# Modulation products of a two-layer diffusion backbone: 512 moving columns instead of four times 128

## The chip, the core and the metric

The kernel runs on one core of one Trainium2 chip. The metric is the device time of one execution in microseconds (us), the median of several runs. A core has five engines with instruction streams of their own: TensorE (PE in the rows; its weight loads are PEld), VectorE (DVE), ScalarE (ACT), GpSimd (POOL) and SyncE (SP, which only issues DMA transfers here). A DMA transfer is issued on an engine's queue and carried out by 16 shared DMA engines.

## What is computed

The reference runs two layers on 512 latent tokens and 256 context tokens of width 1024. Layer 0 mixes tokens by multi-head latent attention, layer 1 by a bidirectional gated linear recurrence; each is followed by a SwiGLU feed-forward part. Both sub-layers of a layer are normed and modulated:

```python
mod_l = jnp.split((jax.nn.silu(c) @ ada_w[i] + ada_b[i])[:, None, :], N_MOD, axis=-1)
mod_c = jnp.split((jax.nn.silu(c_ctx) @ ada_w[i] + ada_b[i])[None, None, :], N_MOD, axis=-1)
a_l = modulate(rms_norm(x, norm1_w[i]), mod_l[0], mod_l[1])
...
x = x + mod_l[2] * o_l
```

The change concerns the first two lines: two vectors (c and c_ctx, width 1024) times a weight matrix `ada_w[i]` of 1024 x 6144, for each of the two layers, in float32. Its 6144 outputs are shifts, scales and gates.

## The kernel before

Activations lie feature-major: a feature tile is 128 features on the 128 partitions, with tokens along the free axis. Most products of the kernel are split by hand into a high and a low part of each factor and taken as three products (`mm3`, lines 93 to 99; `mm3m`, lines 101 to 110); their lines are 97 to 99 and 108 to 110. A weight tile comes through a ring: `weight` (lines 72 to 85) takes a buffer of tag "wf" (1024 columns, four buffers), loads it by a transfer on SP, and makes the high part on ScalarE (L83) and the low part on GpSimd (L84).

The modulation is computed by `ada` (lines 150 to 168), in calls of four chunks of 128 outputs. A layer has 48 chunks, so there are twelve calls a layer and 24 in all. The vectors SiLU(c) and SiLU(c_ctx) lie in `s32`: for each feature tile k of eight, 128 x 32, of which two columns are used. For each chunk i the call takes a buffer of the same ring "wf" and loads 512 KB: all eight feature tiles of one chunk, side by side (L155). Then it makes eight products, one per feature tile (L158): stationary `s32[:, k, :]` with 32 columns, moving 128 columns of the weights, in plain float32, which the chip runs as two instructions. The product of feature tile k writes the 32 partitions that begin at 32 * (k % 4) of the bank, so it uses the strip of 32 array columns with number j = k % 4:

```python
j = k % 4
nc.tensor.matmul(rows_ps[32 * j:32 * j + 32, i * P:(i + 1) * P], lhsT=self.s32[:, k, :],
                 rhs=w[:, k * P:(k + 1) * P], start=(k < 4), stop=(k >= 4))
```

The bank is then copied to SBUF by ScalarE (L161), transposed by TensorE in four pieces (L164), and VectorE sums the four strips and adds the bias (L166, L168).

The calls stand here: four for the first norm of layer 0, while the inputs are loaded (L341, L352, L353); ten spread over the heads of the attention (L543, chunks by `ADA_HEAD`, the last four of them layer 1's); two before the feed-forward part of each layer (L679); two at the first norm of layer 1 (L318); three after the last head of the recurrence (L893, by `ADA_HG`) and one at its output (L854, by `ADA_O`).

The order of each engine's instructions isn't the order of the code. The program is built with `schedule_with_timeline_sim=True` (L1124): a scheduler plays the program through and gives each engine, whenever it would be free, the ready instruction of highest priority. Products of `ada` in the attention have their priority lowered (`PRIO`, "ada_m"), so they are put where the scheduler finds nothing else ready. An engine then runs its own list strictly in the order given, on the chip.

`pack` (lines 1066 to 1113) lays out the inputs on the host. `cols(w, n)` (L1070) cuts a matrix into blocks of n output columns and puts each block's feature tiles side by side; for the modulation n is 128 (L1082), so that a chunk is one block of 512 KB in memory.

Of the kernel before, what the change touches and what calls it, by code (L numbers as in the profile page):

```python
# [17 lines left out]
P = 128  # L18
D = 1024
KD = D // P  # L20
# [22 lines left out]
RING = 1024  # L43
# [12 lines left out]
class Kernel:  # L56
# [93 lines left out]
    def ada(self, l, u0, n, pool, bank):  # L150
        nc = self.nc
        rows_ps = bank()
        for i in range(n):
            w = self.ring.tile([P, RING], F32, tag="wf", name="adaw", bufs=4)
            nc.sync.dma_start(out=w[:, :D], in_=self.a["ADA"][l, u0 + i])  # L155
            for k in range(KD):
                j = k % 4
                nc.tensor.matmul(rows_ps[32 * j:32 * j + 32, i * P:(i + 1) * P], lhsT=self.s32[:, k, :],  # L158
                                 rhs=w[:, k * P:(k + 1) * P], start=(k < 4), stop=(k >= 4))
        rows = pool.tile([P, 512], F32, tag="adarow", name="rows", bufs=1)  # L160
        nc.scalar.copy(rows[:, :n * P], rows_ps[:, :n * P])  # L161
        tp = bank()
        for i in range(n):
            nc.tensor.transpose(tp[:, i * P:(i + 1) * P], rows[:, i * P:(i + 1) * P], self.ident)  # L164
        s = pool.tile([P, 4, 2], F32, tag="adas", name="adas", bufs=2)
        nc.vector.tensor_reduce(s[:, :n], tp[:, :n * P].rearrange("p (u j c) -> p u c j", u=n, j=4)[:, :, 0:2, :], axis=AX.X, op=ALU.add)  # L166
        b = self.vec[:, VEC_AB + l * 48 + u0:VEC_AB + l * 48 + u0 + n]
        nc.vector.tensor_tensor(self.mod[l][:, u0:u0 + n, :], s[:, :n], b.unsqueeze(2).broadcast_to([P, n, 2]), op=ALU.add)  # L168
# [407 lines left out]
    def bank(self, ps):  # L576
        return ps.tile([P, 512], F32, tag="q", name="q", bufs=5)
# [488 lines left out]
def pack(i):  # L1066

    f = {k: np.asarray(v) for k, v in i.items()}

    def cols(w, n):  # L1070

        k, m = w.shape
        return np.ascontiguousarray(w.reshape(k // P, P, m // n, n).transpose(2, 1, 0, 3)).reshape(m // n, P, k // P * n)

    def vec(v):
        return v.reshape(-1, P).T

    d = {}
    xt = np.concatenate([f["x"][0], f["ctx"][0]], 0)
    d["XT"] = np.ascontiguousarray(xt.T.reshape(KD, P, NT).transpose(1, 0, 2))  # L1080
    d["CC"] = np.ascontiguousarray(np.stack([vec(f["c"][0]), vec(f["c_ctx"])], -1))
    d["ADA"] = np.stack([cols(f["ada_w"][l], P) for l in range(2)])  # L1082
    d["VEC"] = np.ascontiguousarray(np.concatenate(
        [vec(f["norm1_w"].ravel()), vec(f["norm2_w"].ravel()), vec(f["ada_b"].ravel()),
         vec(f["hg_lb_logits"].ravel()), f["hg_o_norm_w"][0].reshape(P, 1)], 1))
    d["BC"] = np.concatenate([f["mla_q_norm_w"][0], f["mla_kv_norm_w"][0], f["mla_qn_w"][0], f["mla_kn_w"][0],
                              f["mla_qr_w"][0], f["mla_kr_w"][0]])
    d["WIN"] = np.ascontiguousarray(f["mla_w_in"][0].reshape(KD, P, 704).transpose(1, 0, 2))
    d["WUP"] = np.ascontiguousarray(np.concatenate(
        [cols(f["mla_w_uq"][0], 384), cols(f["mla_w_ukv"][0], 256).reshape(H // 2, 2, P, 512).transpose(0, 2, 1, 3).reshape(H // 2, P, 1024)], 2))  # L1090
    d["MWO"] = cols(f["mla_w_o"][0], P)
    d["W1"] = np.stack([cols(f["ffn_w1"][l], P) for l in range(2)])
    d["W3"] = np.stack([cols(f["ffn_w3"][l], P) for l in range(2)])
    d["W2"] = np.stack([cols(f["ffn_w2"][l], P) for l in range(2)])
    wi = f["hg_w_in"][0]
    d["HW"] = np.stack([cols(wi[:, m * D:(m + 1) * D], P) for m in (0, 1, 2, 4)])
    d["HWI"] = cols(wi[:, 3 * D:4 * D], 256)
    d["HWO"] = cols(f["hg_w_o"][0], P)

    s, t = np.meshgrid(np.arange(32), np.arange(32), indexing="ij")  # L1100
    lv = [s == t] + [(s // (2 * b) == t // (2 * b)) & (s // b != t // b) for b in (1, 2, 4, 8, 16)]
    d["MSK"] = np.ascontiguousarray(np.tile(np.stack(lv, 1), (4, 1, 1)).astype(np.float32))

    row = np.repeat(np.arange(NL // 64, dtype=np.float32), 64)
    col = np.tile(np.arange(64, dtype=np.float32), NL // 64)
    inv = np.power(np.float32(10000.0), -np.arange(0, 32, 2, dtype=np.float32) / np.float32(32)).astype(np.float32)
    ar, ac = row[:, None] * inv, col[:, None] * inv
    ang = np.concatenate([ar, ar, ac, ac], -1)
    cos = np.concatenate([np.cos(ang), np.ones((NC_, DR))], 0)
    sgn = np.tile(np.repeat(np.array([-1.0, 1.0]), 16), 2)  # L1110
    sin = np.concatenate([np.sin(ang) * sgn, np.zeros((NC_, DR))], 0)
    d["ROPE"] = np.ascontiguousarray(np.stack([cos, sin], 1).reshape(TT, P, 2, DR).transpose(1, 0, 2, 3).astype(np.float32))
    return d
# [15 lines left out]
```

## Time and profile before

| what | value |
|---|---|
| median of three runs | 1847.92 us (1844.15 to 1857.01) |
| the profiled execution | 1853.65 us |
| its span, first to last instruction | 1851.9 us |
| TensorE busy | 1755.5 us, 95% of the span |
| VectorE, ScalarE, GpSimd busy | 1016.3, 762.6, 760.6 us |
| mean granted clock of TensorE | 0.982 of full speed |

The rows further down come from the profiled execution. In them L158 is line 158 of the kernel, `out<-in` names the tile written and the tiles read, and x16 the number of instructions that one row sums up. Products are pipelined, so the duration of one holds its way through the array, and rows of the timeline overlap a little. Where an engine sat idle ahead of a row, the idle time and what ended it stand in brackets.

### The profile page before, as it was taken

To read this page: it belongs to the slowest core of one execution; us is meant where nothing else is said; L and a number is where in the kernel's file an instruction comes from. 1 tells how busy PE (TensorE), PEld (TensorE's weight loads), DVE (VectorE), ACT (ScalarE), POOL (GpSimd) and SP (SyncE) were. 2 spreads that over 40 slices of the span, in tenths; PEclk is the share of its full clock that TensorE was granted. 3 is DMA by queue.
4 is the path that set the end of the run, shared out by engine and by line. 5 is a ranking of instruction groups with operands and counts; after the bars stand their busy time and mean duration, and the time that the engine had idled before them with its cause. 6 is when DMAs were issued, how large, how long until landed. Compare 5 with 4: busy or idle time off the path is not lost. (4 is left out here: it accounts for less than half of the span.)

```text
span 1851.9 us, 33106 instructions
## 1 busy us (share of the span) xinstructions
PE 1755.5 (95%) x13708; PEld 1591.8 (86%) x13708; DVE 1016.3 (55%) x1646; ACT 762.6 (41%) x1467; POOL 760.6 (41%) x528
## 2 busy tenths in 40 slices
PE   4889999999899999999999999999998889999999
PEld 3878989788799999988887888888896779999888
DVE  5567887741754445432203666575745278888400
ACT  4355565532554344432213332423333255555411
POOL 2333342216566666643344554554643440000442
PEclk9999999999999999999999999999999989999999
DMA  7412032523222322254224121111115233333331
GB/s 268 137 39 73 25 116 98 170 74 122 103 86 97 104 96 103 81 168 136 86 71 148 60 69 47 61 55 58 58 35 191 94 137 103 103 115 103 108 118 49
DMA packets 55015, 183.61 MB, mean 99 GB/s; under 512 B 6224, under 2 KB 8528, under 8 KB 54864
## 3 DMA queue, kind: packets, MB, share of 16 engines
q1 hardware_dynamic: 53424, 173.62, 28.5%
q10 hardware_dynamic: 1440, 7.86, 1.2%
q8 instruction: 108, 1.77, 0.4%
q14 instruction: 43, 0.35, 0.1%
HBM read 171.50 MB, written 9.96 MB: 98 GB/s over the span
## 5 line engine op out<-in xcount | busy, mean ns | idle before, releaser
L84 POOL TENSOR_TENSOR wl<-wf,wh 128x1024 fp32r<-128x1024 f32 (+2 forms) x130 | 287.0, 2214 | 438.9 <-ACT wh L83 436.5
L83 ACT CAST wh<-wf 128x1024 fp32r<-128x1024 f32 (+2 forms) x130 | 122.9, 947 | 226.2 <-PE L L98 102.5
L97 PE MATMUL q<-op,sh 128*128 128x384 f32 (+1 forms) x640 | 197.3, 310 | 1.0 <-ACT sh L622 1.0
L98 PE MATMUL q<-op,sh 128*128 128x384 f32 (+1 forms) x640 | 197.6, 310 | 0.0
L99 PE MATMUL q<-op,sl 128*128 128x384 f32 (+1 forms) x640 | 194.9, 310 | 0.0
L97 PEld LDWEIGHTS q<-op,sh 128*128 128x128 f32 x640 | 120.3, 188 | 1.5 <-ACT sh L622 1.5
L98 PEld LDWEIGHTS q<-op,sh 128*128 128x128 f32 x640 | 120.3, 188 | 0.0
L99 PEld LDWEIGHTS q<-op,sl 128*128 128x128 f32 x640 | 119.5, 188 | 0.0
L623 POOL TENSOR_TENSOR sl<-wf,sh 128x1024 fp32r<-128x1024 f32 (+1 forms) x40 | 88.7, 2218 | 56.4 <-ACT sh L622 56.4
L98 PE MATMUL L<-op,sh 128*128 128x256 f32 (+1 forms) x360 | 110.4, 307 | 0.0
L99 PE MATMUL L<-op,sl 128*128 128x256 f32 (+1 forms) x360 | 110.3, 306 | 0.0
L97 PE MATMUL L<-op,sh 128*128 128x256 f32 (+1 forms) x360 | 110.3, 306 | 0.0
L1060 DVE TENSOR_TENSOR X<-X,T 128x512 f32<-128x512 f32 x96 | 78.1, 855 | 47.0 <-PE lv L985 45.9
L557 DVE SCALAR_TENSOR_TENSOR xl<-L,mod,xl 128x512 f32<-128x512 f32 x24 | 17.9, 750 | 153.8 <-PE L L99 149.8
L622 ACT CAST sh<-wf 128x1024 fp32r<-128x1024 f32 x80 | 66.7, 834 | 70.2 <-PE L L98 32.7
L98 PE MATMUL L<-f_lo,wh 128*128 128x512 f32 (+1 forms) x240 | 89.1, 371 | 0.0
L97 PE MATMUL L<-f_hi,wh 128*128 128x512 f32 (+1 forms) x240 | 89.0, 371 | 0.0
L99 PE MATMUL L<-f_hi,wl 128*128 128x512 f32 (+1 forms) x240 | 88.5, 369 | 0.0
L158 PE MATMUL L<-adaw,s 128*32 128x128 f32 x1216 | 57.1, 297 | 29.5 <-DMA adaw<-in_ADA 29.3
L975 POOL TENSOR_SCALAR km<-X 128x512 f32<-128x512 f32 x40 | 29.4, 737 | 125.5 <-DVE X L1060 76.4
L622 ACT CAST sh<-sb 128x1024 fp32r<-128x1024 f32 x40 | 42.0, 1050 | 88.5 <-PE q L98 46.6
L158 PEld LDWEIGHTS L<-adaw,s 128*32 128x32 f32 x1216 | 34.8, 116 | 46.1 <-DMA adaw<-in_ADA 17.2
(466 smaller groups left out, 5585.3 us busy)
## 6 DMA issues: line engine op xcount, KB each, us to landing
wf<-in_W SPq DMA_DIRECT2D x104, 512.0 KB, 3.5
adaw<-in_ADA SPq DMA_DIRECT2D x96, 512.0 KB, 4.4
wf<-in_HW SPq DMA_DIRECT2D x32, 512.0 KB, 3.5
wf<-in_W SPq DMA_DIRECT2D x24, 384.0 KB, 3.2
gd<-s SPq DMA_DIRECT2D x10, 768.0 KB, 3.5
g<-gd ACTq DMA_DIRECT2D x10, 768.0 KB, 4.7
wf<-in_W SPq DMA_DIRECT2D x16, 320.0 KB, 3.0
wf<-in_MWO SPq DMA_DIRECT2D x8, 512.0 KB, 4.1
```

What stands on the lines that cost most here:

```text
L83: nc.scalar.copy(hi[:, :n], w[:, :n])
L84: nc.gpsimd.tensor_sub(lo[:, :n], w[:, :n], hi[:, :n].bitcast(F32))
L97: nc.tensor.matmul(out, lhsT=lh, rhs=rh, start=(new and i == 0), stop=False, skip_group_check=more)
L98: nc.tensor.matmul(out, lhsT=lh, rhs=rl, start=False, stop=False, skip_group_check=more)
L99: nc.tensor.matmul(out, lhsT=ll, rhs=rh, start=False, stop=(i == n - 1), skip_group_check=more)
L158: nc.tensor.matmul(rows_ps[32 * j:32 * j + 32, i * P:(i + 1) * P], lhsT=self.s32[:, k, :], rhs=w[:, k * P:(k + 1) * P], start=(k < 4), sto ...
L557: nc.vector.scalar_tensor_tensor(xk, po, gate[:, s:s + 1], xk, op0=ALU.mult, op1=ALU.add)
L622: nc.scalar.copy(hi[:, :n], s)
L623: (nc.vector if j in on_dve else nc.gpsimd).tensor_sub(lo[:, :n], s, hi[:, :n].bitcast(F32))
L975: nc.gpsimd.tensor_scalar(km.rearrange("p (m b r) -> p m b r", b=2, r=L), mix, 1.0, 0.0, op0=ALU.mult, op1=ALU.add)
L1060: nc.vector.tensor_tensor(v, v, t, op=ALU.mult)
```

## The change

The weights are laid out in blocks of 512 output columns, and a call of four chunks is one block. A buffer of the ring now holds two feature tiles of all four chunks in place of eight feature tiles of one chunk. For each feature tile one product takes 512 moving columns. The strip is still k % 4, and the transfers are still four a call with 512 KB each; a partition's part of a transfer is 4 KB in one piece, and the pieces of neighbouring partitions lie 16 KB apart.

```diff
     def ada(self, l, u0, n, pool, bank):
         nc = self.nc
         rows_ps = bank()
-        for i in range(n):
+        g, c0 = divmod(u0, 4)
+        src = self.a["ADA"][l, g].rearrange("p (k c) -> p k c", k=KD)[:, :, c0 * P:(c0 + n) * P]
+        kn = RING // (n * P)
+        for k0 in range(0, KD, kn):
             w = self.ring.tile([P, RING], F32, tag="wf", name="adaw", bufs=4)
-            nc.sync.dma_start(out=w[:, :D], in_=self.a["ADA"][l, u0 + i])
-            for k in range(KD):
+            nc.sync.dma_start(out=w.rearrange("p (k c) -> p k c", k=kn), in_=src[:, k0:k0 + kn])
+            for k in range(k0, k0 + kn):
                 j = k % 4
-                nc.tensor.matmul(rows_ps[32 * j:32 * j + 32, i * P:(i + 1) * P], lhsT=self.s32[:, k, :],
-                                 rhs=w[:, k * P:(k + 1) * P], start=(k < 4), stop=(k >= 4))
+                nc.tensor.matmul(rows_ps[32 * j:32 * j + 32, :n * P], lhsT=self.s32[:, k, :],
+                                 rhs=w[:, (k - k0) * n * P:(k - k0 + 1) * n * P], start=(k < 4), stop=(k >= 4))
...
-    d["ADA"] = np.stack([cols(f["ada_w"][l], P) for l in range(2)])
+    d["ADA"] = np.stack([cols(f["ada_w"][l], 4 * P) for l in range(2)])
```

## Rows read from the trace of the kernel before

**Rows 1.** The page: busy time, share of the span and instructions by engine.

```profile
PE 1755.5 (95%) x13708; PEld 1591.8 (86%) x13708; DVE 1016.3 (55%) x1646; ACT 762.6 (41%) x1467; POOL 760.6 (41%) x528
```

**Rows 2.** Busy by stage: PE, PEld, DVE, ACT, POOL; then clock, DMA share, GB/s.

```profile
0.00:56.00 56.00, 32.20 (x354) 23.93 (x354) 27.14 (x55) 22.58 (x39) 14.06 (x15) 0.94 0.81 270
...
130.00:370.00 240.00, 229.54 (x2027) 203.00 (x2026) 190.22 (x442) 138.13 (x345) 80.90 (x96) 0.98 0.29 100
...
463.00:476.00 13.00, 9.67 (x151) 6.28 (x150) 9.44 (x20) 4.69 (x9) 2.10 (x2) 0.99 0.77 271
...
1395.00:1418.00 23.00, 18.13 (x441) 14.05 (x439) 13.33 (x25) 9.41 (x23) 3.60 (x6) 0.93 0.70 237
```

**Rows 3.** Busy time by stage, L158 alone: PE, then PEld.

```profile
130.00:370.00 240.00, 31.59 (x640) 18.78 (x640) 0.98 0.29 100
...
sum 1852.00, PE 69.91 PEld 43.28; mean PE 5.83 PEld 3.61
```

**Rows 4.** Timeline of TensorE in the attention: start, duration, line, count.

```profile
173.57 0.28 PE L98 MATMUL L<-wl,cn_hi 128*128 128x256 f32 x1
173.69 0.28 PE L99 MATMUL L<-wh,cn_lo 128*128 128x256 f32 x1
173.90 0.41 PE L158 MATMUL L<-adaw,s 128*32 128x128 f32 x2
...
176.18 0.64 PE L158 MATMUL L<-adaw,s 128*32 128x128 f32 x14
177.12 0.41 PE L158 MATMUL L<-adaw,s 128*32 128x128 f32 x2
...
177.93 1.08 PE L158 MATMUL L<-adaw,s 128*32 128x128 f32 x32
...
179.26 0.64 PE L158 MATMUL L<-adaw,s 128*32 128x128 f32 x14
```

**Rows 5.** The same timeline at 353 to 358 us, runs of other lengths.

```profile
353.53 0.42 PE L158 MATMUL L<-adaw,s 128*32 128x128 f32 x6 [0.80 <-DMA adaw<-in_ADA]
...
354.35 0.41 PE L158 MATMUL L<-adaw,s 128*32 128x128 f32 x4
...
357.31 0.62 PE L158 MATMUL L<-adaw,s 128*32 128x128 f32 x10
```

**Rows 6.** Timeline of TensorE at layer 0's second norm.

```profile
468.71 1.13 PE L215 MATMUL q<-dg,ones 128*128 128x512 f32 x2
470.37 0.64 PE L158 MATMUL L<-adaw,s 128*32 128x128 f32 x16 [0.53 <-DMA adaw<-in_ADA]
470.94 0.70 PE L215 MATMUL q<-dg,ones 128*128 128x256 f32 x2
...
474.41 0.65 PE L158 MATMUL L<-adaw,s 128*32 128x128 f32 x16 [2.02 <-DMA adaw<-in_ADA]
474.98 0.62 PE L108 MATMUL q<-op,wh 128*128 128x384 f32 x2
```

**Rows 7.** The first and the last run of L158 in TensorE's timeline.

```profile
17.03 2.28 PE L158 MATMUL L<-adaw,s 128*32 128x128 f32 x32 [17.03 <-DMA adaw<-in_ADA]
...
1493.53 0.64 PE L158 MATMUL L<-adaw,s 128*32 128x128 f32 x16
```

**Rows 8.** Waits of TensorE: us in total, times, longest.

```profile
PE L L158 <- DMA adaw<-in_ADA: 29.3, 11, 17.0
```

**Rows 9.** SP's waits, two DMA issues, and the first transfers' rate (last column).

```profile
SPq L155 <- PE L L158: 102.3, 27, 37.3
...
adaw<-in_ADA SPq DMA_DIRECT2D x96, 512.0 KB, 4.4
...
wf<-in_WIN SPq DMA_DIRECT2D x8, 352.0 KB, 4.0
...
2.00:10.00 8.00, 0.00 (x0) 0.00 (x0) 2.75 (x10) 5.70 (x10) 0.00 (x0) 1.00 0.87 273
10.00:20.00 10.00, 2.85 (x36) 1.97 (x36) 5.58 (x12) 4.68 (x10) 0.00 (x0) 1.00 0.91 324
```

## The prediction, made before the change was run

> **What bounds the kernel now.** I read the page first, then TensorE's busy time by stage, then the order of its instructions around the line that changes, then the waits.
>
> The page has TensorE busy for 95% of the span, no other engine over 55% [rows 1]. So a microsecond that TensorE gains or loses is mostly a microsecond of the kernel, unless it falls where TensorE waits anyway. The products of the change (L158) are 1536 instructions, two for each of 768 float32 products, the two passes over the same columns.
>
> By stage, the attention stretch has TensorE busy 229.5 of 240 us: bound by TensorE. The short stretch at layer 0's second norm, 463 to 476 us, has it busy three quarters of the time, with the DMA engines at 77%: there the modulation weights pace the work. There are six such places, of which three stretches are shown [rows 2]. L158 alone is busy 69.9 us: 31.6 in the attention stretch, for ten of the 24 calls, and 38.3 in the other fourteen [rows 3]. That is 3.16 and 2.74 us a call.
>
> The timeline shows how a call runs. It isn't one block: the scheduler cuts it and puts the pieces between other products. The call at 174 us comes as 2, 14, 2, 32 and 14 instructions [rows 4]. Over the program I count 86 such runs, 3.6 to a call; the first and the last are shown [rows 7]. And the length of a run is a staircase. A run of 2 instructions (one product) takes 0.41 us, of 4 takes 0.41, of 6 takes 0.42; then 10 take 0.62, 14 take 0.64, and 32 take 1.08 [rows 4, 5]. One product and three cost the same. Products of four feature tiles go to four different strips of 32 array columns (j = k % 4 in the code), and the strips work at once; a run lasts as long as the strip with most to do. 16 more instructions, four more per strip, cost 0.44 us.
>
> Is that the streaming of columns, or a price of each instruction? The broadcast product of the norm answers it: two passes over 512 columns take 1.13 us, over 256 columns 0.70 [rows 6]. 0.43 us for 2 x 256 columns is 0.84 ns a column and pass. A strip's four passes over 128 columns at that rate are 0.43 us, and the staircase says 0.44. So L158 is bound by columns streamed per strip, at four strips; loading and issuing are hidden behind it.
>
> **The change, part by part.** It keeps the 24 calls, the 96 transfers of 512 KB, the copy of the rows, the four transposes and the sums. It replaces 32 products of 128 columns per call by 8 of 512. The columns streamed are the same.
>
> *An uncut call.* Before, 64 instructions in one run would take 0.64 + 3 x 0.44 = 1.96 us. After, 16 instructions, two products for each strip: the first four products take 0.41 + 2 x 384 x 0.84 ns = 1.06 us, and four more add 2 x 512 x 0.84 ns = 0.86, in all 1.92. Gain 0.04 us a call, 1 us over 24: nothing.
>
> *A cut call.* Here the change loses. A narrow unit held all eight feature tiles, so every tile that arrived, and every piece of eight products, kept four strips busy. After, a piece of one, two or three wide products keeps one, two or three strips busy, and costs 1.06 us as four would. A weight tile now holds two feature tiles, so a piece of one tile uses half the strips. By pieces per call: one piece 1.92 us; two even pieces 2.12, two uneven ones 1.06 + 1.92 = 2.98; three pieces 3.18; four pieces 4.24.
>
> *How many pieces.* The trace of before cannot show this, since the schedule is worked out anew. From below: one piece. From above: eight, every product alone, 8.5 us a call. The nearest rows are today's 3.6 runs. Runs of a single narrow product [rows 4] may vanish or become a whole wide one; a gap that took 7 or 16 narrow products takes 2 or 4 wide ones. I take 3.5 pieces in the attention stretch: midway between 3.18 and 4.24, 3.71 us, plus 0.3 for waits inside runs, which stay (ten calls, 43 runs by 0.2 and 40 units by 0.44 make 26 of the 31.6 us): 4.0 against 3.16, so +0.85 us a call and +8.5 for ten. A run also costs idle time ahead of it: 0.21 us lie between the start of the product before it and its own, where 0.12 is usual [rows 4], some 0.1 us; eight runs fewer give 0.8 back. That leaves 7.7, and as TensorE is busy 229.5 of 240 us there, a little slack takes some: +6.
>
> *The stretches paced by transfers.* There a run starts when its weights land: TensorE waited 29.3 us for them, 17.0 of it before its first instruction [rows 8]. At 474.41 a unit of 16 runs behind such a wait of 2.02 us, and the layer's first feed-forward product follows it 0.57 us later [rows 6]. After, the last tile of a call holds two wide products: 1.06 instead of 0.64, +0.43 us behind the last landing. The first tile of a call is also released later, by the same 0.43, and the ring of four buffers lets SP issue the next call's transfers only on such releases: SP waited 102 us for L158 [rows 9]. Five places have two or more calls on end at the pace of transfers (two in the first 56 us, then from 463 us, at layer 1's first norm, and from 1395 us; the sixth, layer 1's second norm, is left out since the feed-forward weights follow late there too) [rows 2]. 5 x 0.86 = 4.3, part of it beside the norm's own chain: +4. Queued behind the waiting issue on SP are the weights of the next products, which share the ring; they move by the same 0.4 us.
>
> *The transfers themselves.* As many, as large; a partition's 4 KB stay in one piece, now 16 KB apart in memory. The weights of the input projection are read in rows that lie apart as well and land in 4.0 us, the modulation weights of before in 4.4 [rows 9]. Cost 0; if the pieces were halved to 2 KB, the bound is below.
>
> *Everything else.* 1152 fewer matrix products and as many fewer weight loads to issue: no row shows TensorE waiting for issue in these runs beyond what the staircase holds, so 0. The new durations also reorder the whole schedule around the calls; I have no row for the sign of it and put it into the range, some 5 us either way.
>
> *Sum.* +6 and +4: 10 us. The profiled execution took 1853.65 us for a span of 1851.9, so it would become 1864; it lies 5.7 us above the median of the three runs, 1847.92, to which I refer the forecast: 1858 us.
>
> **The rivals.**
>
> *Torn apart by tile.* Slower. The order waits for each weight tile and puts other products between, as it does with today's units of 16 at 468 to 475 us [rows 6]. Four pieces a call of 1.06 us, two strips idle in each. In the attention stretch 10 x (4.24 + 0.3 - 3.16) = 14; in the other calls 14 x (4.24 + 0.3 - 2.74) = 25, of which the waits for transfers hide about half. 26 to 39 us: 1874 to 1887. It decides from about four pieces a call on. For it: a tile is the unit in which work becomes ready. Against it: four buffers hold a whole call, and in the attention stretch they have mostly landed before a run begins.
>
> *Fewer pieces.* Long products fill a gap that short ones filled in several goes. At two even pieces a call 2.12 + 0.3 = 2.4 us, against 3.16: -7 us in the attention stretch, nothing elsewhere, with the runs saved -9: 1839 (elsewhere the waits for transfers hide it). At one piece everywhere 24 x (2.91 - 2.22) = 17 us less, and 6 for 62 runs fewer: 1825. Against it: what cuts the runs today is other work becoming ready, and that is still there.
>
> *A wide product costs less than four narrow ones.* The change would then do what its form suggests. If a strip's 512 columns took half of what four times 128 take, a call would lose 0.87 us of its 1.74 and 24 calls 21 us: 1827. The row against it is the broadcast product at 0.84 ns a column [rows 6], the same rate as the staircase. The Trainium skill, TensorE: Matmul & The Clock Gate, section "Back-to-back issue gap", gives sustained spacings of about 81 ns for 128 columns and 131 ns for 512, by which a wide product costs 1.6 narrow ones. By that page 24 calls would save about 25 us (estimate), and this case's trace disagrees with it for float32.
>
> *Transfers in pieces of 2 KB.* While the inputs came in 2 KB and 1 KB pieces, the core moved 273 GB/s, with the 4 KB weights 324 [rows 9]. A call's 2.1 MB would take 7.7 instead of 6.5 us; for 14 paced calls at most 17 us: 1865. The layout speaks against it.
>
> **How the numbers follow.** Forecast (about three to four pieces, +2 to +18 us) 0.50; torn apart by tile 0.28; fewer pieces 0.13; wide products cheaper 0.05; smaller transfer pieces 0.04. A measurement of this kernel can tell about 1%, 18.5 us, from no change. Slower by more: the torn case and half of the last, 0.30. Faster by more: cheaper products and the far end of fewer pieces, 0.07. Within: 0.63. The range goes from two even pieces (1839) to the torn case without hiding (1887), less what lies at its ends: 1838 to 1885. The likeliest case alone reaches from 1850 to 1866.
>
> **What would show it.** L158 with 384 products' instructions of 128x512 in place of 1536; runs of 2 to 8 instructions lasting about 1.06 us, of 16 about 1.92. If runs of 16 last near 1.1, the strips did not set the price and I am wrong in the main step. The sum of L158's busy time should rise from 69.9 to about 80; if it falls under 60, the calls run in fewer pieces; if it is near 100, they are torn by tile. The attention stretch should be longer by some 6 us, the stretches at the norms by under 1 each, the feed-forward stretches unchanged. Transfers should land in 4.4 us as before.

## The result, and the profile after

| kernel | median of its runs | ratio to the kernel before, runs of one job | 95% interval |
|---|---|---|---|
| before (12 runs) | 1844.81 us (1839.04 to 1857.01) | 1 | |
| changed (12 runs) | 1861.72 us (1853.01 to 1870.09) | 1.0089 | 1.0065 to 1.0114 |
| changed, later on another chip (e11, 7 runs) | 1859.60 us (1855.82 to 1865.64) | 1.0081 | 1.0051 to 1.0110 |

The change costs 0.8 to 0.9%, 15 to 17 us. The forecast was 1858 us and slower by 10. The profiled execution of the changed kernel took 1868.63 us, 7 us above its own median; that of the kernel before lay 9 us above its median in these runs. So both were profiled a second time (e0 and e11), and what follows rests on what the two profiles of a kernel share. TensorE's mean granted clock was 0.982 and 0.985 of full speed before, 0.984 and 0.985 after: the loss isn't the clock's.

The page of the changed kernel, for [rows 1] and the transfers of [rows 9], and its costliest group of the changed product, which is L161 now (after the arrow: idle time ahead of the group, and what ended most of it):

```profile
PE 1762.3 (94%) x12556; PEld 1560.8 (84%) x12556; DVE 1021.3 (55%) x1646; ACT 763.2 (41%) x1467; POOL 763.4 (41%) x528
...
L161 PE MATMUL L<-adaw,s 128*32 128x512 f32 x304 | 58.1, 629 | 24.5 <-DMA adaw<-in_ADA 24.3
...
adaw<-in_ADA SPq DMA_DIRECT2D x96, 512.0 KB, 4.6
```

1152 instructions fewer, as the change says, and TensorE busy 6.8 us longer (6.7 between the two second profiles). The transfers land in 4.6 us, not 4.4.

TensorE's timeline of the changed kernel, runs of L161:

```profile
44.05 1.05 PE L161 MATMUL M<-adaw,s 128*32 128x512 f32 x4
...
45.70 1.05 PE L161 MATMUL M<-adaw,s 128*32 128x512 f32 x4
...
48.20 1.05 PE L161 MATMUL M<-adaw,s 128*32 128x512 f32 x4
...
173.18 1.92 PE L161 MATMUL L<-adaw,s 128*32 128x512 f32 x16
```

The step costs are those of the forecast to 0.01 us: two products 1.05 (forecast 1.06), eight 1.92 (1.92). A tile that comes alone costs 1.05 where it cost 0.64 [rows 6]. A whole call costs what it did: no call of the kernel before ran uncut, but one of the narrow calls of e4 did, in 1.95 us.

How often a call is cut came out the other way round from the forecast in the attention. The ten calls there ran in 43 pieces before and run in 20 now, 2.0 a call; four of the ten run in one piece. The other fourteen calls, at the transfers' pace, went from 43 to 35 pieces, and 19 of the 35 are single tiles of 1.05 us (one took 1.92 us at the lower clock level). Busy time by stage, columns as in [rows 3]: L158 alone, kernel before (two stages that [rows 3] left out), then L161 alone, changed kernel, in the same stages:

```profile
0.00:56.00 56.00, 12.12 (x256) 7.28 (x256) 0.94 0.81 270
...
1000.00:1015.00 15.00, 5.29 (x128) 3.20 (x128) 1.00 0.72 258
```

```profile
0.00:60.00 60.00, 17.11 (x64) 2.34 (x64) 0.94 0.77 250
...
134.00:374.00 240.00, 26.46 (x160) 4.51 (x160) 0.99 0.31 104
...
1006.00:1022.00 16.00, 6.13 (x32) 0.98 (x32) 1.00 0.73 244
...
sum 1866.00, PE 72.61 PEld 11.79; mean PE 6.05 PEld 0.98
```

In the attention 31.6 us of [rows 3] became 26.5: 5.1 us gained. In the other fourteen calls 69.9 - 31.6 = 38.3 became 72.6 - 26.5 = 46.1: 7.8 us lost, 5.0 of them in the first 60 us. The second profiles have 30.6 and 28.5 us in the attention, 37.4 and 46.8 in the other calls. Two pieces of the 28.5 ran at the lower clock level; with the time lost to that level taken off, the gain in the attention is 4.7 us in the first pair of profiles and 4.1 in the second.

The 5.1 us gained in the attention are not in the kernel's time. All of TensorE's work in that stretch, changed kernel (columns as in [rows 2], where it was busy for 229.5 of 240 us):

```profile
134.00:374.00 240.00, 223.64 (x1533) 186.24 (x1534) 192.86 (x440) 139.65 (x345) 87.34 (x98) 0.99 0.31 104
```

TensorE is busy 5.9 us less in 240 us (5.0 between the second profiles; a little of it because the window holds 14, then 6, other products fewer), and the stretch isn't shorter. What it waits for (us in total, times, longest), first before, then changed, in that stretch:

```profile
PE M L489 <- DVE qk_hi L492: 5.0, 2, 3.7
...
PE sc L514 <- ACT p L524: 0.2, 1, 0.2
```

```profile
PE sc L517 <- ACT p L527: 4.1, 5, 1.9
PE M L492 <- DVE qk_hi L495: 3.2, 3, 1.7
...
PE M L492 <- DVE nm L524: 2.5, 1, 2.5
PE M L492 <- ACT p L527: 1.9, 1, 1.9
PE tp L533 <- DVE pt_lo L536: 1.8, 3, 0.8
```

The wait for qk_hi was there before, and one of 1.9 us for pt_lo too. New or longer are the other waits for the softmax's chain on ScalarE and VectorE (nm, p and pt_lo, L524 to L536). All rows of this view add up to 12.5 us before and 17.7 after, in the second profiles to 9.5 and 15.0: 5.2 and 5.5 us more, about what the pieces gained. In the second profile the waits at L517, L492 for nm and L533 are 3.7, 2.5 and 1.9 us, where e0 has 0.2 and none; that of L492 for p is 1.35 us there, and put down to qk_hi.

Had the narrow pieces stood in these gaps? At six of the waits for nm, p and pt_lo of 0.3 us and more, 7.0 us together, they had: in the kernel before, a narrow piece runs directly ahead of the product that now waits. The longest, before and after:

```profile
338.02 0.85 PE L158 MATMUL L<-adaw,s 128*32 128x128 f32 x22
338.81 0.33 PE L489 MATMUL M<-ident,arena 128*128 128x128 f32 x1
```

```profile
346.27 0.33 PE L492 MATMUL M<-ident,arena 128*128 128x128 f32 x1 [2.46 <-DVE nm L524]
```

Run in larger blocks, the call takes less time, and these gaps stand empty. At three more waits, 3.7 us, no piece had run in the 5 us ahead of the product; these come with the new order of the other products. In the second profiles it is five waits of 5.5 us and three of 3.3.

Where the time went, by stretch: I took the start of each product that both kernels have, subtracted the time lost up to there while the granted clock was at the lower of its two levels, 1.2 GHz (half of TensorE's busy time in those stretches; 29.6 and 22.9 us in all in the two profiles before, 26.8 and 22.1 after), and compared the mean of the two profiles after with the mean of the two before.

| stretch of the kernel before, us | forecast | measured |
|---|---|---|
| start, to 90 | +1.7 | +4.8 |
| attention, to 430 | +6 | +1.6 |
| layer 0's second norm, to 500 | +0.9 | +1.5 |
| feed-forward, to 990 | 0 | -0.6 |
| layer 1's first norm, to 1040 | +0.9 | +2.7 |
| recurrence, to 1385 | 0 | -0.1 |
| last head and output, to 1480 | +0.9 | +3.4 |
| layer 1's second norm, to 1530 | 0 | +3.2 |
| feed-forward, to the end | 0 | +0.9 |
| sum | +10 | +17.4 |

Without the subtraction the spans differ by 1861.0 - 1845.45 = 15.55 us. A single row is good to some 2 us only: at 90 us the two profiles of one kernel lie 4 us apart, so of the single rows only the start, the last head and layer 1's two norms stand clear. The 0.9 of the last row is one execution: 1.9 us in the first profile, none in the second.

How a paced stretch loses, at layer 1's first norm. TensorE's timeline before, then after:

```profile
1006.11 0.43 PE L158 MATMUL L<-adaw,s 128*32 128x128 f32 x8 [2.29 <-DMA adaw<-in_ADA]
1006.47 1.12 PE L215 MATMUL q<-dg,ones 128*128 128x512 f32 x2
...
1007.88 0.70 PE L215 MATMUL q<-dg,ones 128*128 128x256 f32 x2
```

```profile
1011.93 1.05 PE L161 MATMUL L<-adaw,s 128*32 128x512 f32 x4 [2.42 <-DMA adaw<-in_ADA]
...
1013.67 0.66 PE L167 MATMUL M<-ident,rows 128*128 128x128 f32 x4 [0.69 <-ACT rows L164]
1014.16 1.02 PE L218 MATMUL q<-dg,ones 128*128 128x512 f32 x2
1015.12 1.05 PE L161 MATMUL L<-adaw,s 128*32 128x512 f32 x4
1016.10 0.70 PE L218 MATMUL q<-dg,ones 128*128 128x256 f32 x2
```

From the landing of the first call's last tile to the start of the norm's second broadcast product it took 1007.88 - 1006.11 = 1.77 us; now 1016.10 - 1011.93 = 4.17, and 4.17 in the second profile too. Before, the scheduler took half a tile (0.43), then the broadcast product, and let ScalarE's copy of the rows run beside it. Now the tile's two products take 1.05, the copy is waited for (0.69), and another tile's 1.05 stands ahead of the second broadcast product. The piece is longer, and the order around it worse.

### The profile page after: what moved, and what is told of

Its sections match the earlier page's. It is cut to its first block, busy times and chain, and to the rows that moved or that the text cites. A ratio compares the mean times of both kernels' runs of the same rounds, so it can differ in the third digit from the quotient of the medians.

```text
span 1866.8 us, 30803 instructions
## 1 busy us (share of the span) xinstructions
PE 1762.3 (94%) x12556; PEld 1560.8 (84%) x12556; DVE 1021.3 (55%) x1646; ACT 763.2 (41%) x1467; POOL 763.4 (41%) x528
## 5 line engine op out<-in xcount | busy, mean ns | idle before, releaser
L83 ACT CAST wh<-wf 128x1024 fp32r<-128x1024 f32 (+2 forms) x130 | 122.8, 947 | 229.5 <-PE L L98 100.1
L97 PE MATMUL q<-op,sh 128*128 128x384 f32 (+1 forms) x640 | 198.4, 311 | 1.5 <-ACT sh L625 1.5
L99 PE MATMUL q<-op,sl 128*128 128x384 f32 (+1 forms) x640 | 195.2, 310 | 0.0
L97 PEld LDWEIGHTS q<-op,sh 128*128 128x128 f32 x640 | 120.5, 188 | 2.0 <-ACT sh L625 2.0
L99 PEld LDWEIGHTS q<-op,sl 128*128 128x128 f32 x640 | 119.9, 189 | 0.0
L97 PE MATMUL L<-op,sh 128*128 128x256 f32 (+1 forms) x360 | 110.9, 308 | 0.0
L99 PE MATMUL L<-op,sl 128*128 128x256 f32 (+1 forms) x360 | 110.7, 307 | 0.0
L97 PE MATMUL L<-f_hi,wh 128*128 128x512 f32 (+1 forms) x240 | 89.0, 371 | 0.0
L99 PE MATMUL L<-f_hi,wl 128*128 128x512 f32 (+1 forms) x240 | 88.5, 369 | 0.0
L161 PE MATMUL L<-adaw,s 128*32 128x512 f32 x304 | 58.1, 629 | 24.5 <-DMA adaw<-in_ADA 24.3
L97 PE MATMUL L<-gs,wh 128*128 128x512 f32 x180 | 70.4, 392 | 1.7 <-ACT gs L631 1.7
```

The costliest lines, as they stand in the source:

```text
L83: nc.scalar.copy(hi[:, :n], w[:, :n])
L97: nc.tensor.matmul(out, lhsT=lh, rhs=rh, start=(new and i == 0), stop=False, skip_group_check=more)
L99: nc.tensor.matmul(out, lhsT=ll, rhs=rh, start=False, stop=(i == n - 1), skip_group_check=more)
L161: nc.tensor.matmul(rows_ps[32 * j:32 * j + 32, :n * P], lhsT=self.s32[:, k, :], rhs=w[:, (k - k0) * n * P:(k - k0 + 1) * n * P], start=(k ...
```

## The experiments

Three theories stood at first. S: the loss comes from tiles that fill only two of the four strips. W: it comes from the 512 columns themselves. A: it comes from the order that the scheduler works out anew. After the first four runs came D: the rows of a tile, 16 KB apart in memory, cost by themselves. After the second four came C, a collision of two engines at the last head.

**e1: the new layout with narrow products, strip by feature tile.**

```diff
-                j = k % 4
-                nc.tensor.matmul(rows_ps[32 * j:32 * j + 32, :n * P], lhsT=self.s32[:, k, :],
-                                 rhs=w[:, (k - k0) * n * P:(k - k0 + 1) * n * P], start=(k < 4), stop=(k >= 4))
+                for i in range(n):
+                    j = k % 4
+                    nc.tensor.matmul(rows_ps[32 * j:32 * j + 32, i * P:(i + 1) * P], lhsT=self.s32[:, k, :],
+                                     rhs=w[:, ((k - k0) * n + i) * P:((k - k0) * n + i + 1) * P], start=(k < 4 and i == 0), stop=(k >= 4 and i == n - 1))
```

> The layout of after, the products narrow again: 128 columns, 32 to a call, strip still k % 4, so a tile of two feature tiles feeds two strips. Theory S (strips: a tile that feeds two strips takes 1.05 us instead of 0.64 and is released later): as slow as after, ratio to before 1.009 (1.005 to 1.013), runs of 16 instructions last 1.05 us. Theory W (width: a product of 512 columns is a coarse block for the schedule): gone with the width, ratio 1.000 (0.997 to 1.003). Theory A (accident of a rearranged schedule): anywhere from 0.992 to 1.012, in no order with the strips.

Measured: 1891.74 us, ratio 1.0243 (1.0223 to 1.0262). Narrow products alone make it worse. TensorE's timeline of e1, one tile:

```profile
43.98 1.53 PE L162 MATMUL M<-adaw,s 128*32 128x128 f32 x16
```

One tile takes 1.53 us where two wide products on the same two strips take 1.05, since four products of one strip now stand in a row. In the trace the 16 starts form two series of eight, 0.109 us apart in each, and the second series begins 0.47 us after the first, when five of the first have started: across strips the starts aren't in the order of the code.

**e2: the same, each chunk on another strip** (edit against e1; `start` and `stop` go by the first and the last feature tile now).

```diff
-                    j = k % 4
+                    j = (k + i) % 4
...
```

> The same, but the strip is (k + i) % 4 for chunk i, so a tile of two feature tiles feeds all four strips. Theory S: the loss is gone, ratio to before 1.000 (0.997 to 1.003), runs of 16 instructions last 0.64 us, the start stretch is back to the length of before. Theory W: 1.000 too. Theory A: anywhere from 0.992 to 1.012.

Measured: 1858.05 us, 1.0071 (1.0052 to 1.0091). A tile takes 0.64 us again, as before the change. The order of the products over the strips is worth 1.7% (e1 against e2). But with narrow products and four strips, all that the kernel before had, most of the loss is still there: theory W has fallen in its simple form, and S is in doubt.

**e3: half the width, four strips in each tile** (edit against the changed kernel).

```diff
+                for i in range(0, n, 2):
+                    j = (k + i) % 4
+                    nc.tensor.matmul(rows_ps[32 * j:32 * j + 32, i * P:(i + 2) * P], lhsT=self.s32[:, k, :],
+                                     rhs=w[:, ((k - k0) * n + i) * P:((k - k0) * n + i + 2) * P], start=(k < 2), stop=(k >= KD - 2))
```

> Products of 256 columns, 16 to a call, strip (k + i) % 4 for the chunk pair that begins with i: a tile of two feature tiles feeds all four strips. Theory S: 1.000 (0.996 to 1.004), a run of 8 instructions lasts 0.41 + 2 x 128 x 0.84 ns = 0.63 us. Theory W: half of the loss stays, 1.004 or 1.005. Theory A: anywhere from 0.992 to 1.012.

Measured: 1863.56 us, 1.0099 (1.0078 to 1.0119), although a tile takes 0.64 us here too and the costliest group of its products is busy for 50.9 us, less than in any other kernel (all its products of the modulation are busy 63.6 us, where the kernel before has 69.9 and 68.0). Theory S in its simple form has fallen: four strips in each tile don't bring the time back. TensorE as a whole is busy 1754.1 us in e3 and 1755.5 in the first profile of before, at the same mean clock of 0.982, so what e3 loses is waiting and not work.

**e4: a strip for each chunk.** All eight feature tiles of chunk i go to strip i, so nothing is left to sum over strips, and one transpose does for four.

```diff
+                for i in range(n):
+                    nc.tensor.matmul(rows_ps[32 * i:32 * i + 32, :P], lhsT=self.s32[:, k, :],
+                                     rhs=w[:, ((k - k0) * n + i) * P:((k - k0) * n + i + 1) * P], start=(k == 0), stop=(k == KD - 1))
...
-        for i in range(n):
-            nc.tensor.transpose(tp[:, i * P:(i + 1) * P], rows[:, i * P:(i + 1) * P], self.ident)
+        nc.tensor.transpose(tp[:, :P], rows, self.ident)
```

> The layout of after, narrow products, and strip i for chunk i: each strip gathers all eight feature tiles of its chunk, so a call leaves 128 columns in place of 512, one transpose in place of four, and no sum over strips. A tile feeds all four strips. Theory S: the loss is gone and three transposes of 128 columns a call (0.33 us with both passes each) with it: ratio to before 0.997 (0.993 to 1.000). Theory W: the same. Theory A: anywhere from 0.988 to 1.010.

Measured: 1844.94 us, 0.9996 (0.9980 to 1.0012). 72 transposes are gone: TensorE's transposes of the rows are busy 7.5 us, where the two profiles of before have 17.4 and 16.9. That these 9.4 to 9.8 us win nothing against the kernel before suggests that e4 too has a loss to make up, though it has narrow products and four strips. It doesn't prove it, since the attention shows that time which TensorE gains need not be the kernel's.

**e0: the kernel before once more.**

> The kernel before, once more, for a second profiled execution of it. The first one was 8 us above the median of its kernel (1853.65 against 1845). If the first profile is typical in where its time lies, the same stretches last the same here within 1 us each; if the delays read from it were partly its own, a stretch or two of it will be shorter by several us here.

Measured: 1840.78 us. The stretches do not repeat to 1 us: the start is 4.7 us shorter, the time from 1200 to 1450 us 7.6; of the 12.9 us between the two spans 6.7 are the lower clock level. One profile against one other can mislead by nearly as much as the change costs.

**e5, e6, e7: the kernels of the change, of e2 and of e4 with contiguous tiles.** Every engine's list of instructions is the same as without the edit; only the place of the weights in memory differs. The edit in e5:

```diff
-        src = self.a["ADA"][l, g].rearrange("p (k c) -> p k c", k=KD)[:, :, c0 * P:(c0 + n) * P]
...
-            nc.sync.dma_start(out=w.rearrange("p (k c) -> p k c", k=kn), in_=src[:, k0:k0 + kn])
+            nc.sync.dma_start(out=w, in_=self.a["ADA"][l, g, k0 // kn])
...
-    d["ADA"] = np.stack([cols(f["ada_w"][l], 4 * P) for l in range(2)])
+    d["ADA"] = np.stack([np.ascontiguousarray(cols(f["ada_w"][l], 4 * P).reshape(12, P, 4, 1024).transpose(0, 2, 1, 3)) for l in range(2)])
```

> The changed kernel, its instructions in the same order, with each 512 KB tile of the weights stored as one contiguous block in place of 128 rows that lie 16 KB apart. Theory D (the remaining loss comes from the transfers, whose rows lie apart): landing back to 4.4 us or less, time against the kernel before about 1.002 (all of e2's 0.7 per cent gone). Theory A (the loss comes from the rearranged order of the instructions and from the tiles that hold a piece of all four chunks): landing may change by 0.2 us, the time stays at 1.008 to 1.010.

> The kernel of e2 (128 columns, four strips in each tile), with contiguous tiles and nothing else changed. Theory D: 1.000, since strips and products are then those of the kernel before. Theory A: 1.007, as e2.

> The kernel of e4 (a strip for each chunk, one transpose in place of four), with contiguous tiles and nothing else changed. Theory D: 0.993, faster than the kernel before by the 144 transposes that e4 leaves out. Theory A: 1.000, as e4.

Measured: e5 1858.74 us, 1.0059 (1.0038 to 1.0079); e6 1853.73, 1.0030 (1.0010 to 1.0049); e7 1843.32, 0.9972 (0.9951 to 0.9994). Each is 0.2 to 0.4% below its twin, but neither all nor nothing: D is a part. The landing is 4.4 us in e5 and e7, as theory D has it, but 4.6 in e6 as in e2. e7 is faster than the kernel before by 0.3% (0.06 to 0.5%) and than the change by about 1.2%. The 144 transposes of its expectation are 72: 13636 instructions of TensorE against 13708.

**e8: the kernel before with its tiles' rows 16 KB apart.** The reverse test, again with every engine's list unchanged.

```diff
-            nc.sync.dma_start(out=w[:, :D], in_=self.a["ADA"][l, u0 + i])
+            nc.sync.dma_start(out=w[:, :D], in_=self.a["ADA"][l, (u0 + i) // 4][:, (u0 + i) % 4 * D:(u0 + i) % 4 * D + D])
...
-    d["ADA"] = np.stack([cols(f["ada_w"][l], P) for l in range(2)])
+    d["ADA"] = np.stack([cols(f["ada_w"][l], P).reshape(12, 4, P, D).transpose(0, 2, 1, 3).reshape(12, P, 4 * D) for l in range(2)])
```

> The kernel before with its instructions in the same order, and only the place of the weights in memory changed: the 128 rows of a tile lie 16 KB apart, as in the changed kernel, in place of one block. Theory D (rows that lie apart cost by themselves): 1.002 to 1.005, landing up from 4.3 or 4.4 us to 4.6 or more, and TensorE waiting longer for the modulation weights in the first 60 us. If it is 1.000 with the same landing, the 0.3 per cent between e5 and the changed kernel is something else.

Measured: 1855.46 us, 1.0041 (1.0021 to 1.0062). Its page:

```profile
L158 PE MATMUL L<-adaw,s 128*32 128x128 f32 x1216 | 56.5, 296 | 30.7 <-DMA adaw<-in_ADA 30.5
...
adaw<-in_ADA SPq DMA_DIRECT2D x96, 512.0 KB, 4.7
```

and that of its twin, the kernel before (e0):

```profile
L158 PE MATMUL L<-adaw,s 128*32 128x128 f32 x1216 | 55.2, 291 | 26.3 <-DMA adaw<-in_ADA 25.8
...
adaw<-in_ADA SPq DMA_DIRECT2D x96, 512.0 KB, 4.3
```

The products are the same; the transfers land 0.3 to 0.4 us later, and TensorE stands idle longer ahead of them (29.5 us in the first profile of before). D is shown. Over the pairs that differ in this alone (change and e5, e2 and e6, e4 and e7, e9 and e10, e8 and before) the price is 0.30, 0.41, 0.24, 0.11 and 0.41%: 0.29% in the mean, 5.4 us, good to some 2.5 us by the runs' intervals (an estimate). Alone, only the second and the last pair are clear of zero. The Trainium skill, DMA: Bandwidth & Descriptors, section "Latency and other measured facts", reports row pitches of 4 MiB and 8 MiB that halve the rate, while one of 512 KiB nearly keeps it, and advises to pad the pitch or to lay tiles out contiguously. No run here has such a pitch; at 16 KB contiguous tiles still gain, by far less.

**e9, e10: the collision at the last head.** TensorE's wait there is long in the changed kernel:

```profile
1428.16 0.26 PE L997 MATMUL at<-X 128*32 128x32 f32 x1 [4.51 <-DVE X L1063]
```

It is 4.5 us in the first profile, 3.8 in the second, 4.4 in e5 and 4.1 in e3. The first profile of before has 2.3 us there; e0, e2 and e6 have none. VectorE's and GpSimd's timelines of e11, then both of e0:

```profile
1413.94 4.98 DVE L1063 TENSOR_TENSOR X<-X,T 128x512 f32<-128x512 f32 x2 [1.16 <-PE lv L988]
...
1421.25 5.58 DVE L1063 TENSOR_TENSOR X<-X,T 128x512 f32<-128x512 f32 x2
...
1428.09 1.29 DVE L1063 TENSOR_TENSOR X<-X,T 128x512 f32<-128x512 f32 x2 [1.26 <-PE at L998]
```

```profile
1413.24 7.91 POOL L84 TENSOR_TENSOR wl<-wf,wh 128x1024 fp32r<-128x1024 f32 x3
```

```profile
1406.78 1.29 DVE L1060 TENSOR_TENSOR X<-X,T 128x512 f32<-128x512 f32 x2 [1.46 <-PE lv L985]
...
1409.05 4.63 DVE L1060 TENSOR_TENSOR X<-X,T 128x512 f32<-128x512 f32 x2
...
1415.88 3.49 DVE L1060 TENSOR_TENSOR X<-X,T 128x512 f32<-128x512 f32 x2
```

```profile
1407.88 8.05 POOL L84 TENSOR_TENSOR wl<-wf,wh 128x1024 fp32r<-128x1024 f32 x3 [1.76 <-ACT wh L83]
```

The first pair of these three takes 4.98 us beside GpSimd's low parts and 1.29 in e0, where the low parts start later. But e0 collides as well, one pair further on: 4.63 and 3.49 us. The edit holds the three low parts back by one small GpSimd instruction that reads what the pair has written. The other lists stay as they were, but for three output products (L97 to L99) that the scheduler gave other places in TensorE's list around the wait, which the expectation below leaves out:

```diff
...
-            nc.gpsimd.tensor_sub(lo[:, :n], w[:, :n], hi[:, :n].bitcast(F32))
+            with self.tc.issue_after(after.ins) if after else nullcontext(): nc.gpsimd.tensor_sub(lo[:, :n], w[:, :n], hi[:, :n].bitcast(F32))
...
-                    w = self.weight("HWO", (n,), 0, 1024, place)
+                    w = self.weight("HWO", (n,), 0, 1024, place, self.grown if n < 3 else None)
...
                 T = self.grow(X, T, L, tmp)
+        if h == H - 1: self.grown = nc.gpsimd.tensor_scalar(tmp.tile([P, 1], F32, tag="mark", name="mark", bufs=1), X[:, 0, 0:1], 1.0, 0.0, op0=ALU.mult, op1=ALU.add)
```

> The changed kernel, every engine's order kept, with one instruction of one element put into GpSimd's list: it reads X after the last head's fifth pair of products on VectorE, and so holds back the three low parts of output weights (L84) that ran beside that pair. Theory C (a collision: VectorE's pair takes 4.97 us beside GpSimd's low parts and 1.29 alone, and the head's chain and TensorE wait for it): the pair at 1.3 us, TensorE's wait at L997 from 4.5 to about 1 us, 2 to 4 us off the changed kernel: 1.007. If the cost only moves on to TensorE waiting for the low parts: pair 1.3, a new wait at L99 of 2 to 4 us, time as the changed kernel's, 1.009. If the pair was slow for another reason, it stays near 5 us.

> The same instruction put into the kernel of e5 (changed kernel, contiguous tiles). If D and C add up: 1.0059 less 0.001 to 0.002, so about 1.004. If C only moves the cost: 1.006.

Measured: e9 1858.74 us, 1.0070 (1.0044 to 1.0095); e10 1856.83, 1.0059 (1.0037 to 1.0081). VectorE's timeline of e9, the three pairs that e11 shows above, and TensorE's wait:

```profile
1413.38 1.29 DVE L1063 TENSOR_TENSOR X<-X,T 128x512 f32<-128x512 f32 x2 [1.16 <-PE lv L988]
...
1417.02 3.58 DVE L1063 TENSOR_TENSOR X<-X,T 128x512 f32<-128x512 f32 x2
...
1424.79 3.76 DVE L1063 TENSOR_TENSOR X<-X,T 128x512 f32<-128x512 f32 x2 [4.19 <-PE at L998]
```

```profile
1414.73 0.22 PE L997 MATMUL at<-X 128*32 128x32 f32 x1 [0.83 <-DVE X L1063]
```

The collision is real: the pair is back at 1.29 us, the wait at 0.83. But it is worth nothing that could be measured: e9 stands 0.1% from e11, e10 nowhere from e5. These times alone can't rule out the 2 to 4 us that were expected, since their intervals are as wide; the traces say more. From the start of the first pair to the end of the third it takes 1428.55 - 1413.38 = 15.2 us in e9 and 1429.38 - 1413.94 = 15.4 in e11. The low parts now run beside the next pairs, as they do in e0, and the chain ends where it ended.

**e11: the changed kernel once more.**

> The changed kernel once more, on the same chip as the three above, for a second profiled execution and a comparison without a change of chip: 1.009 again (1.0065 to 1.0114). What its delay against the kernel before repeats from the first profile belongs to the kernel (the collision at L997 above all, since the order is fixed), what does not (part of the 1.9 us lost along layer 1's feed-forward part, part of the start) to the execution.

Measured: 1859.60 us, 1.0081 (1.0051 to 1.0110). The collision, the new waits in the attention and the longer pieces repeat; the 1.9 us in the last feed-forward part don't, and the start costs 2.7 us where the first profile had 6.8 (each against the mean of the two profiles before).

What the runs settle: some 5.4 us of the loss are rows that lie apart. The rest, 1.0059 with contiguous tiles in e5 and e10 (11 us), is the wide products' own longer pieces, the new order of everything around them, or both; how it divides stays open. Two runs say that the order can weigh much. e6, with narrow products and four strips, keeps 1.0030; its interval touches that of e5. And e3, whose pieces are no more work for TensorE than those of the kernel before, still loses 1.0099, about 0.7% of it beyond the price of rows that lie apart. No run changes the order and nothing else.

## Why the prediction was right, and where it was not

*The result.* 1861.72 against 1858, inside the range and inside "about three to four pieces, +2 to +18 us"; slower by less than a measurement of 1% can tell, the likeliest of the three. That the number came out this near is in part luck: two of its terms were wrong by 4 and by 11 us, one each way.

*The staircase* was right. The price is the columns of the busiest strip, not the instruction: 1.05 and 1.92 us, as worked out. So was what follows from it, that an uncut call gains nothing (1.95 us narrow, in e4). "A wide product costs less than four narrow ones" fell with it.

*"How many pieces"* is the step that failed. I took 3.5 pieces a call in the attention and +6 us; they are 2.0, and L161 is busy 4 to 5 us less there, not 8 more. The rival "fewer pieces" had this count right, its gain nearly (-7 at two pieces) and the time wrong: the stretch came out no shorter (1.6 us longer, within the 2 us that a row is good for), since TensorE now waits for the softmax chain, at six places where a narrow piece had run. Both took TensorE's busy 229.5 of 240 us as proof that its time is the stretch's. My reading is that it was so busy because the filler was fine enough. That the gaps returned is read from the waits of both profiles; no run isolates it. The sign that I named, L158's busy time in all, came out at 72.6 and 75.2 us, between the 80 of the forecast and the 60 of fewer pieces: the attention's fewer pieces and the other calls' longer ones nearly cancel in it.

*"The stretches paced by transfers"* had the mechanism and the wrong size: +4 forecast, 15.6 measured in the table's five paced rows, of which up to 5.4 belong to the next point. I charged 0.43 us for the last tile and for the first release of five places. In fact 19 of the pieces in the fourteen paced calls are single tiles at 1.05 against 0.64, and L161's busy time in the fourteen calls rose by 7.8 us. The place that I left out, layer 1's second norm, lost 3.2: its last call now comes as

```profile
1497.88 1.05 PE L161 MATMUL L<-adaw,s 128*32 128x512 f32 x4 [1.09 <-DMA adaw<-in_ADA]
...
1499.92 1.05 PE L161 MATMUL L<-adaw,s 128*32 128x512 f32 x4
1501.13 1.05 PE L161 MATMUL L<-adaw,s 128*32 128x512 f32 x4 [0.15 <-DMA adaw<-in_ADA]
...
1502.55 1.05 PE L161 MATMUL L<-adaw,s 128*32 128x512 f32 x4
```

four pieces of one tile each: the rival "torn apart by tile". It holds in the stretches where tiles arrive one by one; in the attention it holds for one call of ten, at 316 us.

*"The transfers themselves", cost 0,* was wrong by 5.4 us. The row I leaned on, input weights that lie apart and land in 4.0 us, is of 352 KB; scaled to 512 KB it would have been 5.8, and said nothing against a price.

*The sum.* 7.8 us of longer pieces in the paced calls, 5.4 of transfers and 1.6 in the attention make 14.8, beside 15 to 17 measured; an estimate, since the first two overlap where TensorE waits for a landing. That the sum fits doesn't show its parts: e3 has none of the 7.8 us, and loses as much. Two errors of opposite sign (the attention too dear by 4, the paced stretches with their transfers too cheap by 11) left the forecast 7 us short.

## What to carry to other kernels

Work that a scheduler uses to fill gaps has a size that matters: cut coarser it may take less of the engine's time and still not shorten the kernel, because gaps that it filled stand empty; look at what the engine would wait for without it before counting its busy time as gain. Where products run on strips of the array, what a piece costs is the columns of its busiest strip, so let every unit that can arrive alone hold work for all strips, in an order that alternates between them; e3 warns that this alone need not bring the kernel's time back, once the order of everything else is new. And when a layout is changed for the products' sake, keep each transfer's source in one block: test it alone, with the instructions unchanged.

## What the runs showed of the hardware that was not expected

How far products on different strips overlap depends on their order in the code. One tile's columns took 1.53 us as 16 instructions with eight of one strip in a row (e1), 1.05 as two wide products, one on each of two strips (the changed kernel), and 0.64 as 16 instructions with four strips in turn (e2).

VectorE's product of two tensors slows down beside GpSimd's difference of two: 1.29 us a pair alone, and 3.5 to 5.6 beside it. The Trainium skill, SBUF — State Buffer, section "SBUF: two separate sides", says that a VectorE instruction with two inputs in SBUF and a GpSimd instruction that reads SBUF exclude each other for the whole instruction. The rows fit: in e11's pair of 4.98 us each product took (4.98 - 1.29) / 2 = 1.84 us longer, less than one low part of 7.91 / 3 = 2.6 us.
